# A macaron encoder block on one core: norms after the sub-layers computed in place by VectorE, four tiles at a time, and small constants loaded later

## The chip, the cores and the metric

The kernel runs on one core of one Trainium2 chip. The metric is the device time of one execution in microseconds; the median of three runs is compared, and one execution is also profiled. All data are float32 in HBM. The engines are named as in the profile: PE (TensorE), DVE (VectorE), ACT (ScalarE), POOL (GpSimd) and SP (SyncE, which here only issues DMAs).

## The reference, cut to what matters

```python
def rms_norm(x, g):
    y = x * lax.rsqrt(jnp.mean(x * x, axis=-1, keepdims=True) + EPS)
    return y * g
def swiglu(x, w_gate, w_up, w_down):
    return (jax.nn.silu(x @ w_gate) * (x @ w_up)) @ w_down
# 1024 tokens, 1024 channels, 2816 hidden
f1 = swiglu(rms_norm(h, ffn1_pre_g), ffn1_w_gate, ffn1_w_up, ffn1_w_down)
h = h + 0.5 * rms_norm(f1, ffn1_post_g)
mix = hybrid_mixer(rms_norm(h, mix_pre_g), ...)   # latent attention + dilated attention, gated, w_out
h = h + rms_norm(mix, mix_post_g)
f2 = swiglu(rms_norm(h, ffn2_pre_g), ffn2_w_gate, ffn2_w_up, ffn2_w_down)
h = h + 0.5 * rms_norm(f2, ffn2_post_g)
```

## The kernel before, in words

The 1024 tokens are eight tiles of 128 rows, t0 to t7. Every float32 product is made of three fp32r products (high by high, high by low, low by high), so each operand exists as a rounded "high" part and a "low" rest. Both FFNs use a seven-product Strassen scheme, so the input to gate and up is seven blocks of 512 tokens by 512 channels: four quarters and sums of them.

**The norms.** `prenorm` squares a tile on ACT with a running sum, makes 1/sqrt of the mean on POOL in two tiny instructions (`rstd_steps`: `var` L309, `rstd` L311), and scales the tile by that and by the gain (L453). How many of the 1024 columns DVE scales is the constant PRE1, PREM or PRE2 (768, 768 or all); the others are scaled by ACT (L459) and multiplied by the gain on POOL (L460). `postnorm` loads the residual, squares y on ACT (L501), multiplies y by the gain into a new tile `xn` (L490; the first columns on POOL, by the tables POOL1, POOLM and POOL2, the others on DVE), and then adds `xn` times rstd to the residual on DVE (L514). At two of the three places `prenorm` of the next sub-layer follows at once on the same tile; `norm_tok` lets two tiles through this pair at a time.

**Transposes.** A normed tile is transposed by PE in groups of four 128x128 pieces into one PSUM bank (L428), then ACT rounds it to `xh` (L432) and DVE makes the rest `xl` (L433), which frees the bank. There are four such banks; products use them too. For the FFNs, `XS.put` makes the sums of token halves on DVE (L416) when a tile of the second half arrives, into two `xt` tiles, and these are transposed as well. A second-half tile thus costs four L416 and five groups of transposes, a first-half tile two groups.

**What sets the order.** The program is written by generators that ask a planner (`Plan`) for an engine with an estimated duration and a rank; the planner runs its own clock and calls the code that emits each instruction. The tile framework then lists the instructions by engine, each engine runs its list in order, and every load is on SP's one queue. Loads that depend on nothing late come far ahead of where the text has them.

**Places that the change touches.** `begin` loads x and spawns the norms of the first FFN: tile 0, then 1 to 3, then 4 to 7 after a wait of 12 units of the planner's clock. `last_evac` (L1171) adds the last two products of an FFN's down projection to the accumulator `acc`; `post1` then runs the two norms into the mixer's input. `merge` makes the output projection (evacuated at L2560 into `y`) and `tail` runs the norms into the second FFN. `post2` is the last norm, whose result goes to the output. `tables`, `latent`, `dilated` and `merge` load small constants: 16 KB of masks and frequencies (`cst`), 4 KB of positions (`posi`, 4-byte pieces), the gains of the latent norms (`gq_home`), selection matrices (`sels`) and the gate bias (`bg`).

```python
        m = split_at
        spawn(on_dve(0, 512, scaled[0]), rank)
        if m > 512:
            spawn(on_dve(512, m, scaled[1]), rank)
        if m < D:
            spawn(on_pool(m, D, scaled[1]), rank)
```

Of the kernel before, what the change touches and what calls it, by code (L numbers as in the profile page):

```python
# [107 lines left out]
PRE1, PREM, PRE2 = 768, 768, D  # L108
POOL1, POOLM, POOL2 = [512] * 8, [384] * 8, [512] * 4 + [1024, 768, 512, 512]
# [4 lines left out]
EARLY = 4  # L114
W0 = 4
# [106 lines left out]
def _build(tc, es, a, consts, out, dbg):  # L222
# [44 lines left out]
    def act(n, fn):  # L267
        return ("act", 0.04 + n * 0.00088, fn)
# [87 lines left out]
    class XS:  # L356
# [25 lines left out]
        def put(self, t, xn, scaled, rank):  # L382
# [15 lines left out]
            else:  # L398
# [14 lines left out]
                tt = [slot([P, 2, 512], name="xt") for _ in range(2)]  # L413
                t1, t2, t3, t4 = tt[0][:, 0, :], tt[0][:, 1, :], tt[1][:, 0, :], tt[1][:, 1, :]
# [21 lines left out]
    def prenorm(src, g, X, t, rank, split_at, xn=None):  # L436

        bx, rs = [], []

        def sq():  # L440
            sq_ = slot([P, D], name="xn") if xn is None else xn
            ssq = small([P, 1], name="ssq")
            A.activation(sq_, src, AF.Square, accum_out=ssq)
            bx.extend((sq_, ssq))

        yield act(D + 100, sq)
        yield from rstd_steps(bx[1], D, rs)
        xn = bx[0]
        m = split_at
        scaled = [Event(), Event((m > 512) + (m < D))]  # L450

        def on_dve(c0, c1, ev):
            yield dve(c1 - c0, lambda: V.scalar_tensor_tensor(  # L453
                xn[:, c0:c1], src[:, c0:c1], rs[0], g()[:, c0:c1], op0=ALU.mult, op1=ALU.mult,
            ))
            plan.set(ev)

        def on_pool(c0, c1, ev):
            yield act(c1 - c0, lambda: A.mul(xn[:, c0:c1], src[:, c0:c1], rs[0]))  # L459
            yield pool(c1 - c0, lambda: G.tensor_mul(xn[:, c0:c1], xn[:, c0:c1], g()[:, c0:c1]))  # L460
            plan.set(ev)

        spawn(on_dve(0, 512, scaled[0]), rank)
        if m > 512:
            spawn(on_dve(512, m, scaled[1]), rank)
        if m < D:
            spawn(on_pool(m, D, scaled[1]), rank)
        yield from X.put(t, xn, scaled, rank)
# [4 lines left out]
    def postnorm(y, g, res_src, dst, t, box, junk, pool_cols, parts=1):  # L473
# [10 lines left out]

        m = pool_cols(t)
        gained = Event((m > 0) + (m < D))

        def gain_of(cols, eng):
            def write():
                eng.tensor_mul(xn[:, cols], y[:, cols], g()[:, cols])  # L490

            n = cols.stop - cols.start
            yield (pool if eng is G else dve)(n, write)
            plan.set(gained)

        xn = slot([P, D], name="xn")
        box.append(xn)
# [6 lines left out]
        if m:  # L504
            spawn(gain_of(slice(0, m), G), 0)
        if m < D:
            spawn(gain_of(slice(m, D), V), 8)
        yield act(D + 100, sq)
        yield from rstd_steps(bx[0], D, rs)
        yield gained  # L510
        n = D // parts
        for q in range(parts):
            cs = slice(n * q, n * q + n)
            yield dve(n, lambda: V.scalar_tensor_tensor(res[:, cs], xn[:, cs], rs[0], res[:, cs], op0=ALU.mult, op1=ALU.add))  # L514
            spawn(store(dst[t * P : (t + 1) * P, cs], res[:, cs], 512 // parts), 6)
# [708 lines left out]
    def begin():  # L1224
        def one(t):
            bx = []

            def ld():
                xt = slot([P, D], name="x")
                load(xt, a["x"][t * P : (t + 1) * P, :])  # L1230
                bx.append(xt)

            yield dma(512, ld)
            yield gains0
            yield from prenorm(bx[0], lambda: gb["g1"], X1, t, 3, PRE1)
# [6 lines left out]
        yield 12.0  # L1242
# [5 lines left out]
    norm_tok = Tokens(2)  # L1248

    def post1(y, t):  # L1250
# [8 lines left out]
        yield from postnorm(y, lambda: gb["p1"], a["x"], h1, t, bx, lambda: gb["j1"], POOL1.__getitem__)  # L1259
        yield from prenorm(bx[0], lambda: gb["gm"], Xm, t, 3, PREM, bx[1])  # L1260
# [8 lines left out]
    def tables():  # L1269
# [3 lines left out]
        def fetch():  # L1273
            load(cst[:, P:], consts[:, C_MJ:C_END])
            posi = keep([P, NT], I32, "posi")
            load(posi, a["positions"][0:1, :].rearrange("o (t p) -> p (o t)", p=P))
            bx.posi = posi
# [319 lines left out]
    def latent():  # L1597
# [3 lines left out]
        def lg():  # L1601
            load(gq[:, 0:384], a["q_norm_g"][0:1, :].broadcast_to([P, 384]))
# [723 lines left out]
    def dilated():  # L2326
# [3 lines left out]
        def ld():  # L2330
            dc.sel = keep([P, 2, P], F32, "sels")
            load(dc.sel, consts[:, C_SEL:C_MJ].rearrange("p (c n) -> p c n", c=2))
            dc.b1 = slot([P, 3, 256], name="b1")
            load(dc.b1, consts[:, C_B1:C_B23].rearrange("p (n c) -> p n c", c=256))
            dc.b23 = gq_home[:, 0:512].rearrange("p (n c) -> p n c", c=256)
# [118 lines left out]
    def merge():  # L2454
        yield ob_done
        bg = keep([P, 16], F32, "bg")
        yield dma(10, lambda: load(bg, a["b_gate"][0:1, :].rearrange("o (c p) -> p (o c)", p=P)))
# [106 lines left out]
        def tail(y, t, ev):  # L2564
# [3 lines left out]
            yield from postnorm(y, lambda: gb["pm"], h1, h2, t, bx, lambda: gb["jm"], POOLM.__getitem__)  # L2568
            yield from prenorm(bx[0], lambda: gb["g2"], X2, t, 3, PRE2, bx[1])
# [50 lines left out]
    def post2(y, t):  # L2620
# [5 lines left out]
        yield from postnorm(y, lambda: gb["p2"], h2, out, t, [], lambda: gb["j2"], POOL2.__getitem__, 2 if t == NT - 1 else 1)  # L2626
# [40 lines left out]
```

## Time and profile before

| what | value |
|---|---|
| time, median of 3 runs | 2434.36 us (2431.82 to 2435.98) |
| time of the profiled execution | 2432.88 us |
| its span, first to last instruction | 2430.7 us |
| PE, DVE, ACT, POOL busy | 94%, 66%, 43%, 32% of the span |
| mean granted TensorE clock | 0.974 |
| instructions | 30689 |
| moved by DMA | 350.17 MB, mean 144 GB/s |

The profile is of one execution. Engines are busy when an instruction runs on them; the granted clock is a share of full speed, 1.0 being the higher of the two levels. A bracket at the end of a line of the timeline is the idle time of the engine before that instruction and who ended it. The profiled execution took 2432.88 us, of which 2430.7 us are the span.

### The profile page before, as it was taken

How to read it: one execution, taken by the hardware profiler on the slowest of the kernel's cores; microseconds unless marked ns; L12 is line 12 of the kernel's file. 1: busy time of each engine (PE TensorE's matmuls, PEld its weight loads, DVE VectorE, ACT ScalarE, POOL GpSimd, SP SyncE). 2: the span in 40 equal slices, each digit the busy share in tenths (PEclk: the TensorE clock that was granted, in tenths of full speed). 3: DMA queues.
4: the chain of work that ended last, by engine and by line, in shares of the span. 5: the costliest groups of instructions: out<-in, count | busy, mean ns of one | idle time of the engine just before them, and what ended most of it. 6: DMA issues, size and time to landing. Idle time of an engine off the chain costs nothing. (4 is left out here: it accounts for less than half of the span.)

```text
span 2430.7 us, 30689 instructions
## 1 busy us (share of the span) xinstructions
PE 2294.6 (94%) x11096; PEld 1920.7 (79%) x11096; DVE 1609.8 (66%) x2669; ACT 1044.0 (43%) x1952; POOL 784.1 (32%) x592
## 2 busy tenths in 40 slices
PE   6999999999979999999998898988979999999997
PEld 4788888788869987888886777776868888887885
DVE  7877878875672105666666766347787778778658
ACT  6233434431153336666655545454433334344111
POOL 2000000354274555756532322575300000006443
PEclk9999999999989999999999999999979999999998
DMA  6234434587352133122223222675533444357762
GB/s 186 83 130 139 173 127 163 195 321 254 134 173 70 62 98 100 38 72 65 61 82 90 79 73 85 194 258 180 182 108 113 163 140 173 116 197 280 259 238 104
DMA packets 197145, 350.17 MB, mean 144 GB/s; under 512 B 32577, under 2 KB 112961, under 8 KB 196481
## 3 DMA queue, kind: packets, MB, share of 16 engines
q1 hardware_dynamic: 196992, 348.21, 42.6%
q8 instruction: 87, 1.43, 0.2%
q14 instruction: 66, 0.53, 0.1%
HBM read 234.78 MB, written 113.38 MB: 143 GB/s over the span
## 5 line engine op out<-in xcount | busy, mean ns | idle before, releaser
L706 PE MATMUL s<-xh,wt 128*128 128x512 f32 x1408 | 453.8, 393 | 10.2 <-DVE uu L807 9.0
L524 POOL TENSOR_TENSOR wdb<-rawd,wdb 128x1024 fp32r<-128x1024 f32 x34 | 87.3, 2567 | 892.4 <-ACT wdb L523 889.3
L706 PE MATMUL b<-xh,wt 128*128 128x512 f32 x1056 | 345.7, 394 | 0.7 <-ACT xh L432 0.6
L706 PEld LDWEIGHTS s<-xh,wt 128*128 128x128 f32 x1408 | 266.2, 189 | 69.8 <-DVE uu L807 10.7
L706 PE MATMUL s<-xl,wt 128*128 128x512 f32 x704 | 275.7, 392 | 0.0
L706 PEld LDWEIGHTS b<-xh,wt 128*128 128x128 f32 x1056 | 200.9, 190 | 44.0 <-ACT xh L432 1.0
L706 PE MATMUL b<-xl,wt 128*128 128x512 f32 x528 | 207.7, 393 | 0.9 <-DVE xl L433 0.9
L1134 PE MATMUL b<-wdb,ha 128*128 128x512 f32 x864 | 202.5, 389 | 0.0
L1134 PE MATMUL s<-wdb,ha 128*128 128x512 f32 x816 | 190.5, 389 | 0.0
L1134 PEld LDWEIGHTS b<-wdb,ha 128*128 128x128 f32 x864 | 162.4, 188 | 33.8
L1134 PEld LDWEIGHTS s<-wdb,ha 128*128 128x128 f32 x816 | 153.1, 188 | 31.8
L1495 PE MATMUL b<-xh,wh 128*128 128x512 f32 x384 | 162.7, 424 | 1.4 <-DVE o L2016 0.8
L1966 POOL TENSOR_TENSOR p<-p,rd 128x1024 f32<-128x1024 f32 x64 | 122.5, 1923 | 117.7 <-DVE rd L1963 112.5
L706 PEld LDWEIGHTS s<-xl,wt 128*128 128x128 f32 x704 | 133.3, 189 | 27.4
L1495 PE MATMUL b<-xl,wh 128*128 128x512 f32 x384 | 153.2, 399 | 0.0
L675 ACT CAST wt<-s 128x512 fp32r<-128x512 f32 x176 | 104.2, 617 | 113.9 <-DVE s L635 59.0
L1495 PE MATMUL b<-xh,wl 128*128 128x512 f32 x384 | 152.9, 398 | 0.0
L524 POOL TENSOR_TENSOR wdb<-td,wdb 128x1024 fp32r<-128x1024 f32 x40 | 108.1, 2706 | 109.7 <-ACT wdb L523 98.6
L428 PE MATMUL b<-cst,p 128*128 128x128 f32 x768 | 107.2, 280 | 22.2 <-DVE ptd L433 14.9
L524 POOL TENSOR_TENSOR wl<-raw,wh 128x512 fp32r<-128x512 f32 (+3 forms) x88 | 110.0, 1267 | 53.5 <-ACT wh L523 46.5
L428 PEld LDWEIGHTS b<-cst,p 128*128 128x128 f32 x768 | 90.1, 143 | 40.0 <-DVE ptd L433 17.5
L676 DVE TENSOR_TENSOR wt<-s,wt 128x512 fp32r<-128x512 f32 x176 | 117.9, 684 | 5.4 <-ACT wt L675 5.1
(298 smaller groups left out, 4989.8 us busy)
## 6 DMA issues: line engine op xcount, KB each, us to landing
hs_d<-hl SPq DMA_DIRECT2D x112, 512.0 KB
ha<-hs_d SPq DMA_DIRECT2D x56, 1024.0 KB
raw<-in_ffn_w_gate_dram SPq DMA_DIRECT2D x48, 512.0 KB
raw<-in_ffn_w_up_dram SPq DMA_DIRECT2D x48, 512.0 KB
rawd<-in_ffn_w_down_dram SPq DMA_DIRECT2D x44, 512.0 KB
raw<-in_w_in_dram SPq DMA_DIRECT2D x28, 512.0 KB
h<-res SPq DMA_DIRECT2D x16, 512.0 KB
lg_d<-lg SPq DMA_DIRECT2D x32, 256.0 KB
```

Source lines behind the costliest of these rows:

```text
L428: T.transpose(b[:rows, i * P : (i + 1) * P], src(i), ident)
L524: yield pool(n, lambda: G.tensor_sub(lo, src, hi))
L675: yield act(512, lambda: A.copy(w[:, 0], src))
L676: yield dve(512, lambda: V.tensor_sub(w[:, 1], src, w[:, 0]))
L706: T.matmul(out(), l, r, start=(first and k == 0 and n == 0), stop=(k == 3 and n == 2), skip_group_check=True,)
L1134: T.matmul(ps, l, r, start=(fresh and n == 0), stop=(n == 5), skip_group_check=True)
L1495: T.matmul(bs.ps, l, r, start=(part == 0 and n == 0), stop=(part == 7 and n == 2))
L1966: yield pool(S, lambda: G.tensor_tensor(bx.p, bx.p, bx.rd.broadcast_to([P, S]), op=ALU.mult))
```

## The change

The norms lose their shares for POOL and ACT. `postnorm` multiplies y by the gain in place, all 1024 columns on DVE, after the square on ACT has read y; the tile that was y then takes the next `prenorm`'s result, so no `xn` tile is taken. `prenorm` scales two halves of 512 columns on DVE. `norm_tok` goes from 2 to 4. `XS.put` writes the first and last of its four sums over the old tile and takes one `xt` tile where it took two. Five loads of small constants get a one- or two-column copy ahead of them, from data that come late, into their own destination, so that they cannot be listed early. `begin` spawns tiles 4 to 7 after 7 units in place of 12.

```diff
-PRE1, PREM, PRE2 = 768, 768, D
-POOL1, POOLM, POOL2 = [512] * 8, [384] * 8, [512] * 4 + [1024, 768, 512, 512]
+NORM = 4
...
-                tt = [slot([P, 2, 512], name="xt") for _ in range(2)]
-                t1, t2, t3, t4 = tt[0][:, 0, :], tt[0][:, 1, :], tt[1][:, 0, :], tt[1][:, 1, :]
+                tt = slot([P, 2, 512], name="xt")
+                t1, t2, t3, t4 = old[0], tt[:, 0, :], tt[:, 1, :], old[1]
...
-        def on_pool(c0, c1, ev):
-            yield act(c1 - c0, lambda: A.mul(xn[:, c0:c1], src[:, c0:c1], rs[0]))
-            yield pool(c1 - c0, lambda: G.tensor_mul(xn[:, c0:c1], xn[:, c0:c1], g()[:, c0:c1]))
-            plan.set(ev)
...
+        for n in range(2):
+            spawn(scale(512 * n, 512 * n + 512, scaled[n]), rank)
...
-        if m:
-            spawn(gain_of(slice(0, m), G), 0)
-        if m < D:
-            spawn(gain_of(slice(m, D), V), 8)
+        def gain_of():
+            yield dve(D, lambda: V.tensor_mul(y, y, g()))
+            plan.set(gained)
+
         yield act(D + 100, sq)
+        spawn(gain_of(), 2)
...
-            yield dve(n, lambda: V.scalar_tensor_tensor(res[:, cs], xn[:, cs], rs[0], res[:, cs], op0=ALU.mult, op1=ALU.add))
+            yield dve(n, lambda: V.scalar_tensor_tensor(res[:, cs], y[:, cs], rs[0], res[:, cs], op0=ALU.mult, op1=ALU.add))
...
-        yield 12.0
+        yield 7.0
...
-    norm_tok = Tokens(2)
+    norm_tok = Tokens(NORM)
...
+            seen = X1.blk[6][0].bitcast(F32)[:, 0, 0:1]
+            V.tensor_copy(cst[:, P : P + 1], seen)
             load(cst[:, P:], consts[:, C_MJ:C_END])
             posi = keep([P, NT], I32, "posi")
+            V.tensor_copy(posi[:, 0:1], seen)
...
+            V.tensor_copy(gq[:, 383:385], gb["gm"][:, 0:2])
...
-            load(dc.sel, consts[:, C_SEL:C_MJ].rearrange("p (c n) -> p c n", c=2))
             dc.b1 = slot([P, 3, 256], name="b1")
             load(dc.b1, consts[:, C_B1:C_B23].rearrange("p (n c) -> p n c", c=256))
+            V.tensor_copy(dc.sel[:, 0, 0:1], dc.b1[:, 0, 0:1])
+            load(dc.sel, consts[:, C_SEL:C_MJ].rearrange("p (c n) -> p c n", c=2))
...
+            V.tensor_copy(bg[:, 0:1], dc.sel[:, 0, 0:1])
```

SP at the start of the program, before. The first `x` row is t3, the others are t4 to t7; `raw` are weights of the first FFN.

```order
L1230 DMA x_108<-in_x_dram 128x1024
L519 DMA raw_117<-in_ffn_w_gate_dram 128x8x128
L1274 DMA cst<-in_consts_dram 128x32
L1276 DMA posi<-in_positions_dram 128x8x1
L1602 DMA gq_home<-in_q_norm_g_dram 128x384
L519 DMA raw_163<-in_ffn_w_up_dram 128x8x128
L1230 DMA x_183<-in_x_dram 128x1024
L1230 DMA x_197<-in_x_dram 128x1024
L1603 DMA gq_home<-in_kv_norm_g_dram 128x256
L1230 DMA x_211<-in_x_dram 128x1024
L1230 DMA x_230<-in_x_dram 128x1024
```

The same place in the changed program, from the fourth tile of x on:

```order
L1209 DMA x_108<-in_x_dram 128x1024
L1209 DMA x_117<-in_x_dram 128x1024
L1209 DMA x_135<-in_x_dram 128x1024
L1209 DMA x_159<-in_x_dram 128x1024
L1209 DMA x_178<-in_x_dram 128x1024
L498 DMA raw_190<-in_ffn_w_gate_dram 128x8x128
L498 DMA raw_228<-in_ffn_w_up_dram 128x8x128
L498 DMA raw_259<-in_ffn_w_gate_dram 128x8x128
```

The eight tiles of x stand together, ahead of all weights, and none of the small loads stands near them: `cst` and `posi` come after three and six larger weight loads, `gq_home` some 165 rows later, `sels` and `bg` some 350.

DVE at the end of the first FFN, before. `acc` are the accumulators of two halves (each tile needs two L1171), L490 the gain, L514 the residual, L453 the next norm.

```order
L1171 TENSOR_TENSOR acc_3857<-acc_3857,b_5068 128x512
L490 TENSOR_TENSOR xn_5168<-acc_3847,p_738_5058 128x512
L1171 TENSOR_TENSOR acc_3857<-acc_3857,b_5076 128x512
L514 SCALAR_TENSOR_TENSOR res_5132<-xn_5168,rstd_5187,res_5132 128x1024
L1171 TENSOR_TENSOR acc_3870<-acc_3870,b_5085 128x512
L453 SCALAR_TENSOR_TENSOR xn_5144<-res_5122,rstd_5210,gm_5093 128x512
L1171 TENSOR_TENSOR acc_3870<-acc_3870,b_5095 128x512
L453 SCALAR_TENSOR_TENSOR xn_5144<-res_5122,rstd_5210,gm_5093 128x256
L1171 TENSOR_TENSOR acc_3881<-acc_3881,b_5103 128x512
```

The changed program there (L1150 is the old L1171, L483 the gain, L493 the residual, L451 the next norm, L432 the old L433):

```order
L493 SCALAR_TENSOR_TENSOR res_5124<-acc_3839,rstd_5179,res_5124 128x1024
L1150 TENSOR_TENSOR acc_3882<-acc_3882,b_5126 128x512
L1150 TENSOR_TENSOR acc_3882<-acc_3882,b_5138 128x512
L493 SCALAR_TENSOR_TENSOR res_5136<-acc_3852,rstd_5192,res_5136 128x1024
L1150 TENSOR_TENSOR acc_3891<-acc_3891,b_5154 128x512
L1150 TENSOR_TENSOR acc_3891<-acc_3891,b_5169 128x512
L451 SCALAR_TENSOR_TENSOR acc_3820<-res_5104,rstd_5201,gm_5075 128x512 x2
L451 SCALAR_TENSOR_TENSOR acc_3829<-res_5114,rstd_5225,gm_5075 128x512 x2
L451 SCALAR_TENSOR_TENSOR acc_3839<-res_5124,rstd_5232,gm_5075 128x512 x2
L432 TENSOR_TENSOR xl_5238<-b_5240,xh_5236 128x4x128
L451 SCALAR_TENSOR_TENSOR acc_3852<-res_5136,rstd_5248,gm_5075 128x512 x2
```

All sixteen additions to the accumulators now stand ahead of the first L451, with the gains and residuals of t0 to t3 between them; then come four L451 pairs together, then eight `xl`. Before, the L453 of t0 and t1 stood between the additions, and tiles went on in pairs. PE's list follows: 32 transposes, 96 products, 32 transposes where there were 16, 48, 16, 48, 16, 48.

PE where the second FFN's products meet the first transposes of t4 to t7, before. `wo` by `mt` is the output projection, L706 the second FFN's products.

```order
L285 MATMUL b_15267<-wo_15106,mt_15065 128x512 x3
L706 MATMUL b_15284<-xh_14662,wt_14972 128x512
L706 MATMUL b_15284<-xl_14663,wt_14972 128x512
L706 MATMUL b_15284<-xh_14662,wt_14972 128x512 x2
L706 MATMUL b_15284<-xl_14663,wt_14972 128x512
```

The changed program from the end of its twelfth such product to the transposes (L685 is the old L706, L427 the old L428):

```order
L685 MATMUL b_15137<-xh_14606,wt_15099 128x512 x2
L685 MATMUL b_15137<-xl_14607,wt_15099 128x512
L685 MATMUL b_15137<-xh_14606,wt_15099 128x512
L427 MATMUL b_15342<-cst,y_14591 128x128 x4
L427 MATMUL b_15351<-cst,y_14656 128x128 x4
```

Behind the last output projection stood 36 L706, four transposes and twelve more L706; now twelve stand there, and 36 have gone ahead of the last 48 products of the output projection. Outside these stages and the last norm the lists of PE are the same, instruction for instruction, but for buffer numbers.

## Rows read from the trace of the kernel before

**Rows 1.** Parts 1 and 2 of the page: busy time by engine; clock in 40 slices.

```profile
PE 2294.6 (94%) x11096; PEld 1920.7 (79%) x11096; DVE 1609.8 (66%) x2669; ACT 1044.0 (43%) x1952; POOL 784.1 (32%) x592
...
PEclk9999999999989999999999999999979999999998
```

**Rows 2.** Stretches: length, busy PE, PEld, DVE, ACT, POOL; clock, DMA share, GB/s.

```profile
0.00:58.00 58.00, 36.40 (x162) 26.79 (x162) 45.56 (x76) 36.47 (x68) 14.63 (x28) 0.91 0.62 185
58.00:450.00 392.00, 391.05 (x1723) 322.71 (x1722) 303.15 (x517) 146.99 (x263) 0.00 (x0) 1.00 0.40 139
...
664.00:750.00 86.00, 68.97 (x393) 61.87 (x392) 63.68 (x73) 40.34 (x77) 60.73 (x63) 0.92 0.43 143
...
1660.00:1705.00 45.00, 36.03 (x160) 29.04 (x159) 37.88 (x37) 26.73 (x47) 33.77 (x29) 0.92 0.61 207
...
1763.00:1798.00 35.00, 21.35 (x93) 16.14 (x92) 31.45 (x48) 13.71 (x25) 5.13 (x6) 0.61 0.45 157
...
2391.50:2430.70 39.20, 22.82 (x97) 17.60 (x95) 32.48 (x36) 9.21 (x16) 24.01 (x24) 0.84 0.43 161
```

**Rows 3.** Timeline of SP's queue at the start: start us, us, instruction.

```profile
7.49 3.68 SPq L1602 DMA_DIRECT2D gq_home<-in_q_norm_g_dram  x1
...
11.69 1.18 SPq L1230 DMA_DIRECT2D x<-in_x_dram  x2
```

**Rows 4.** DVE and PE at the start: timeline, and one group of DVE's.

```profile
10.50 1.60 DVE L453 SCALAR_TENSOR_TENSOR xn<-x,rstd,g 128x512 f32<-128x512 f32 x2 [1.99 <-POOL rstd L311]
...
57.62 0.60 PE L428 MATMUL b<-cst,xt 128*128 128x128 f32 x4
...
61.28 0.17 DVE L1286 CAST posf<-posi 128x8 f32<-128x8 int32 x1
...
L453 DVE SCALAR_TENSOR_TENSOR xn<-x,rstd,g 128x512 f32<-128x512 f32 x8 | 8.2, 1025 | 8.9 <-POOL rstd L311 8.9
```

**Rows 5.** Timeline of POOL, DVE and PE at the end of the first FFN.

```profile
666.60 0.69 DVE L1171 TENSOR_TENSOR acc<-acc,b 128x512 f32<-128x512 f32 x1
...
675.88 1.28 DVE L514 SCALAR_TENSOR_TENSOR res<-xn,rstd,res 128x1024 f32<-128x1024 f32 x1 [0.40 <-POOL rstd L311]
...
675.94 3.48 POOL L524 TENSOR_TENSOR wl<-raw,wh 128x1024 fp32r<-128x1024 f32 x1
...
680.37 2.82 DVE L453 SCALAR_TENSOR_TENSOR xn<-res,rstd,gm 128x512 f32<-128x512 f32 x1 [2.61 <-POOL rstd L311]
...
683.85 8.73 PE L285 MATMUL b<-wdb,hp 128*128 128x512 f32 x30 [3.69 <-DVE acc L1171]
...
747.35 2.48 DVE L433 TENSOR_TENSOR xl<-b,xh 128x512 fp32r<-128x512 f32 x4
```

**Rows 6.** A group by shape, 664 to 752 us: count, busy us, mean ns.

```profile
L524 POOL TENSOR_TENSOR wc<-raw,wc 128x768 fp32r<-128x768 f32 x4 | 7.9, 1998 | 0.0
```

**Rows 7.** The mixer's end: a group (1660 to 1705 us), then the timeline.

```profile
L453 DVE SCALAR_TENSOR_TENSOR xn<-res,rstd,g 128x512 f32<-128x512 f32 x8 | 13.0, 1660 | 2.4 <-POOL rstd L311 2.3
...
1752.99 0.39 PE L706 MATMUL b<-xh,wt 128*128 128x512 f32 x1
...
1757.48 3.95 POOL L311 TENSOR_TENSOR rstd<-var,neg_half 128x1 f32<-128x1 f32 x1
...
1782.44 1.09 PE L428 MATMUL b<-cst,xn 128*128 128x128 f32 x4 [8.12 <-DVE xn L453]
...
1793.45 0.78 PE L706 MATMUL b<-xh,wt 128*128 128x512 f32 x1
```

**Rows 8.** Timeline of DVE in the last norm: first addition, last residual.

```profile
2393.07 0.69 DVE L1171 TENSOR_TENSOR acc<-acc,b 128x512 f32<-128x512 f32 x1
...
2425.86 1.42 DVE L514 SCALAR_TENSOR_TENSOR res<-xn,rstd,res 128x512 f32<-128x512 f32 x2 [0.72 <-POOL rstd L311]
```

**Rows 9.** By line and by tile: b1's load; the first use of sels.

```profile
L2334 SPq DMA_DIRECT2D b<-in_consts_dram x1: 385/385/385, 1181.7 to 1181.7; - x1
...
L2169 PE MATMUL b<-z,sels x16: 218/275/323, 1238.1 to 1513.4; 128*128 128x64 f32 x16
```

More of the change, by code (lines that the diff above doesn't have):

```diff
@@ L434, in transpose_split, with prenorm @@
         plan.release(B1)
-    def prenorm(src, g, X, t, rank, split_at, xn=None):
+    def prenorm(src, g, X, t, rank, xn=None):
         bx, rs = [], []
@@ L448, in prenorm, with scale @@
         xn = bx[0]
-        m = split_at
-        scaled = [Event(), Event((m > 512) + (m < D))]
-        def on_dve(c0, c1, ev):
+        scaled = [Event(), Event()]
+        def scale(c0, c1, ev):
             yield dve(c1 - c0, lambda: V.scalar_tensor_tensor(
@@ L456, in on_dve @@
             plan.set(ev)
-        def on_pool(c0, c1, ev):
-            yield act(c1 - c0, lambda: A.mul(xn[:, c0:c1], src[:, c0:c1], rs[0]))
-            yield pool(c1 - c0, lambda: G.tensor_mul(xn[:, c0:c1], xn[:, c0:c1], g()[:, c0:c1]))
-            plan.set(ev)
-        spawn(on_dve(0, 512, scaled[0]), rank)
-        if m > 512:
-            spawn(on_dve(512, m, scaled[1]), rank)
-        if m < D:
-            spawn(on_pool(m, D, scaled[1]), rank)
+        for n in range(2):
+            spawn(scale(512 * n, 512 * n + 512, scaled[n]), rank)
         yield from X.put(t, xn, scaled, rank)
@@ L471, in store, with postnorm @@
         yield dma(kb, lambda: load(dst, src))
-    def postnorm(y, g, res_src, dst, t, box, junk, pool_cols, parts=1):
+    def postnorm(y, g, res_src, dst, t, box, junk, parts=1):
         bx, rs = [], []
@@ L483, in postnorm @@
         res = box[0]
[L485 to L497, printed above, removed]
+        box.append(y)
+        gained = Event()
         def sq():
@@ L502, in sq @@
             bx.append(ssq)
-        if m:
-            spawn(gain_of(slice(0, m), G), 0)
-        if m < D:
-            spawn(gain_of(slice(m, D), V), 8)
+        def gain_of():
+            yield dve(D, lambda: V.tensor_mul(y, y, g()))
+            plan.set(gained)
         yield act(D + 100, sq)
+        spawn(gain_of(), 2)
         yield from rstd_steps(bx[0], D, rs)
@@ L1234, in one @@
             yield gains0
-            yield from prenorm(bx[0], lambda: gb["g1"], X1, t, 3, PRE1)
+            yield from prenorm(bx[0], lambda: gb["g1"], X1, t, 3)
         spawn(one(0), 0)
@@ L1258, in post1 @@
         bx = []
-        yield from postnorm(y, lambda: gb["p1"], a["x"], h1, t, bx, lambda: gb["j1"], POOL1.__getitem__)
-        yield from prenorm(bx[0], lambda: gb["gm"], Xm, t, 3, PREM, bx[1])
+        yield from postnorm(y, lambda: gb["p1"], a["x"], h1, t, bx, lambda: gb["j1"])
+        yield from prenorm(bx[0], lambda: gb["gm"], Xm, t, 3, bx[1])
         plan.release(norm_tok)
@@ L2456, in merge, with ld @@
         bg = keep([P, 16], F32, "bg")
-        yield dma(10, lambda: load(bg, a["b_gate"][0:1, :].rearrange("o (c p) -> p (o c)", p=P)))
+        def ld():
+            V.tensor_copy(bg[:, 0:1], dc.sel[:, 0, 0:1])
+            load(bg, a["b_gate"][0:1, :].rearrange("o (c p) -> p (o c)", p=P))
+        yield dma(10, ld)
         m_tok, w_tok, wd_tok = Tokens(4), Tokens(1), Tokens(4)
@@ L2567, in tail @@
             bx = []
-            yield from postnorm(y, lambda: gb["pm"], h1, h2, t, bx, lambda: gb["jm"], POOLM.__getitem__)
-            yield from prenorm(bx[0], lambda: gb["g2"], X2, t, 3, PRE2, bx[1])
+            yield from postnorm(y, lambda: gb["pm"], h1, h2, t, bx, lambda: gb["jm"])
+            yield from prenorm(bx[0], lambda: gb["g2"], X2, t, 3, bx[1])
             plan.release(norm_tok)
@@ L2625, in post2 @@
         yield gains2
-        yield from postnorm(y, lambda: gb["p2"], h2, out, t, [], lambda: gb["j2"], POOL2.__getitem__, 2 if t == NT - 1 else 1)
+        yield from postnorm(y, lambda: gb["p2"], h2, out, t, [], lambda: gb["j2"], 2 if t == NT - 1 else 1)
     def second():
```

## The prediction, made before the changed kernel was run

> **What bounds the kernel now.** I read the page first. PE is busy for 2294.6 of 2430.7 us, and the clock falls only in a few slices [rows 1]: time can come only from stretches where PE waits or runs at the lower level of its clock. The busy time by stretches shows them [rows 2]. From 58 to 450 us PE is busy for 391.05 of 392 us, 1723 matmuls, 0.227 us each; nothing done there by other engines can show. At the start 21.6 of 58 us are idle, at the end of the first FFN 17.0 of 86, in the output projection 9.0 of 45, at the entry to the second FFN 13.7 of 35 at a clock of 0.61, and in the last norm PE is done before DVE. In all five DVE is the busiest or near it: 45.56 of 58, 63.68 of 86, 37.88 of 45, 31.45 of 35, 32.48 of 39.2 us. These are the five stages where norms stand between two pieces of PE's work. Everything else keeps its order, so the sum is made over these stages.
>
> **Prices.** On DVE, 512 columns cost 0.60 us in a row of such instructions (four in 2.48 us) and 1024 columns 1.28 us alone [rows 5]; I take 1.2 in a row, and 0.64 for half of a scaled tile. The new gain of 1024 columns does not exist in the trace; between twice the 0.60 and the 1.28 there is little to choose. These are times without POOL beside them. With it, the same 512 columns take 1.025 us in the mean at the start [rows 4], 1.66 us at the end of the mixer [rows 7], and once 2.82 us [rows 5]. So the shares that POOL loses shorten what stays on DVE, but POOL's weight splits (3.48 us [rows 5], 2.00 us [rows 6]) and its tiny rstd instructions stay.
>
> **The start: 0.** Eight tiles of x come together. Before, t4 and t5 were issued at 11.69 us, behind small loads, one of which held the queue for 3.68 us [rows 3]. But the data are not the limit: DVE is. The second tile's scaling starts at 10.50 us [rows 4]; from there to the last `xl` of the first FFN's input the changed list of DVE has 64 instructions, at 0.62 us 39.7 us, so the input is complete at 50.2. PE pays for this: its list now puts 88 transposes ahead of the first product, which starts when DVE is 48 instructions on, at 40.3. Then come 20 products and 24 transposes, 4.5 and 3.6 us at full clock (transposes at the 0.15 of four in 0.60 [rows 4]) and twice that at the lower level: PE is through between 48.4 and 56.5 us, but not before the input is. I take 51. At 57.6 us, where PE had become continuous with 49 products done (counted in its old list) [rows 4], it would have 20 + 6.6/0.227 = 49. That is 0; the ends are -2.1 and +5.7 us.
>
> **End of the first FFN: -4.** The first L1171 starts at 666.60 [rows 5]. DVE's list then has 16 L1171 and 2 more additions (10.8 us), four gains and four residuals (9.6), eight L453 (5.1) and eight `xl` (4.8): 30.3 us, with 2 us of waits for squares and rstd the first half of the mixer's input is ready at 699. The second half is 9.6 + 5.1 + 4.8 = 19.5 us: 718.5 if POOL is silent, or 726 if two `wc` splits and one `wl` (2.0 + 2.0 + 3.48) hold DVE up in full, as they are listed just there. PE runs through from about 2 us before that. What PE then lacks to where it stood when the old `xl` ended (747.35 + 2.48 = 749.8 [rows 5]) are 72 products of 256 columns, 96 of 384 and 12 transposes: 8.2 + 16.3 + 1.3 = 25.8 us by 0.227 per 512. So 742.3 or 749.8, against 749.8: -7.5 or 0. I take -4, since the splits overlap only partly with the gains. What goes: the stall of 3.69 us that came when DVE waited 2.61 us for an rstd behind a 3.48 us split [rows 5], because no L453 now stands ahead of an addition. What is late next: the first half, as four tiles must be through before PE's first transposes. Ends: -10.5, if half of the 6.9 us that the clock of 0.92 costs over 86 us [rows 2] goes too, and +4.6, if each of the eight L453 pairs waits another 0.6 us for its rstd, as DVE does at L514 for 0.40.
>
> **Output projection and entry to the second FFN: -2.5.** In the first half DVE's eight L453 took 13.0 us where 5.1 would do [rows 7], partly for POOL's gain shares, which go, partly for its splits, which stay; I give PE back half of its 9.0 idle us [rows 2], -4.5. At the entry, PE ended the output projection at 1752.99 and stood 8.12 us for a tile whose norm had no token [rows 7]; with four tokens that wait goes. But 36 products of the second FFN are now listed ahead of the last 48 of the output projection, 36 x 0.227 = 8.2 us, so y is complete that much later. From there DVE has two residuals, a gain, eight L453, sixteen L416, twenty `xl` and two more: with waits for squares some 34 us, where it took 40.5 from 1752.99 to the first product after the transposes at 1793.45 [rows 7]. 8.2 later and 6.5 shorter is +1.7; another 0.3 for rstds gives +2. Together -2.5, ends -9 (all of the projection's idle time) and +5.
>
> **The last norm: -0.5.** From 2393.07 [rows 8] DVE has 18 additions (10.8 us), eight gains and eight residuals (19.2): 30.0 us, so 2423.1, plus 0.6 for the first square and three waits of 0.72 for rstds, as the last one had: 2425.9. Before, it ended at 2425.86 + 1.42 = 2427.3. That is -1.4; as the last stores now come closer together, I take -0.5, with ends -4 and +2.
>
> **The copies: 0.** Five copies of one or two columns, at most the 0.17 us of a small cast [rows 4], and each makes SP wait for DVE. The loads behind `cst` and `posi` are third and later units' weights, hidden under the continuous stretch; `sels` follows `b1`, issued at 1181.7, and is first used at 1238.1 [rows 9]. If that cover were gone, a load and a copy would show, some 3 us.
>
> **Sum.** 0 - 4 - 2.5 - 0.5 = -7 us. The sum is against the profiled execution, 2432.88 us (span 2430.7), which lies 1.5 us under the median of 2434.36. So 2426 us. About 0.2%, 4.9 us, is what a measurement of this kernel can tell: faster is below 2429.5, slower above 2439.2.
>
> **Rivals.** *Nothing gained.* DVE carries what POOL and ACT carried and the groups of four only move the waits: PE stands longer before the first transposes of each group and shorter later. For it: DVE was the busiest engine in each stage already [rows 2]. Against: it was busy partly because POOL held it. With the weak ends (0 at the first FFN, 0 at the output projection, +2 at the second FFN, 0 at the end): 2435.
>
> *The rstds starve: slower.* One `rstd` took 3.95 us [rows 7] where I take 0.6 for one with DVE idle: it stood through a row of DVE instructions that read two SBUF tiles. Now DVE runs more such rows: gains, residuals and scalings back to back. POOL's rstd then comes late, and DVE itself waits for it at the next residual. There are five groups of tiles (two after each of two sub-layers, and the end) in each of which two rstds can be on the path; if half of the ten lose 3.4 us, that is 17 us, less the gain of 7: 2443. It decides from a mean loss of 0.7 us for each of the ten. Against it: once DVE waits, POOL is free to go on, and additions and `xl`, which read PSUM, stand between in the first halves. The Trainium skill, SBUF — State Buffer, section "Who interferes with whom", says that a VectorE instruction with two SBUF inputs and a GpSimd instruction that reads SBUF exclude each other, and that the one that comes second waits for the whole of the first. The 3.95 us show a wait through more than one instruction; by the rule's single wait, at 1.28 us, the ten would lose 12.8 us at most, and this rival would end at 2438.7.
>
> *All of the freed time arrives.* Without POOL's shares the scalings fall back to 0.64 us, chains end early and the clock stays up. Half of the 17.0 and all of the 9.0 idle us, and 3.5 of the clock's: 2432.88 - 8.5 - 9 - 3.5 = 2412. For it: 1.66 against 0.64 us [rows 7]. Against: the splits stay.
>
> **How the numbers follow.** The forecast, 2419 to 2431, has 0.39; nothing gained 0.27; starving 0.16; all arrives 0.18. Faster by over 0.2% is 0.18, most of the forecast (0.33) and a little of the second case: 0.53. Within 0.2%: 0.06 + 0.23 = 0.29. Slower: 0.16 and 0.02 of the second: 0.18. The range is 2410 to 2441 us: it reaches to the cases on both sides and leaves out the sums of all ends, 2407 and 2450.
>
> **What would show it.** Right: the scalings of 512 columns at 0.6 to 0.75 us in all stages; the input of the first FFN complete near 50 us and PE's first product near 40; no stall for an addition between 664 and 690 us; POOL free of `xn`. Wrong: `rstd` at over 1.4 us in the mean, DVE idle before residuals for more than 2 us a group, PE waiting over 8 us ahead of the first transposes at the end of the first FFN, or a time above 2431 with stages at or above their old length. A time under 2419 would mean that the splits on POOL cost DVE less than I let them.

## The result, and the profile after

The changed kernel takes 2418.99 us (median of four runs, 2418.78 to 2423.56) against 2435.17 of before in the same comparison: a ratio of 0.9941, interval 0.9923 to 0.9958, faster by 0.6%. The forecast was 2426 (2410 to 2441), faster. The profiled execution took 2419.11 us with a span of 2417.3: 13.4 us less span than before, where the sum said 7.

Part 1 of the page after, and the clock:

```profile
PE 2293.5 (95%) x11096; PEld 1920.7 (79%) x11096; DVE 1605.0 (66%) x2675; ACT 1038.5 (43%) x1936; POOL 736.5 (30%) x552
...
PEclk9999999999989999999999999999989999999999
```

DVE is no busier than before, though it has taken over columns from POOL and ACT [rows 1]: POOL lost 48 us, and DVE got back in shorter instructions what it took on: its busy time is 1605.0 us, 1609.8 before. Busy time by stretches of the kernel after, with the columns of [rows 2], each stretch set to hold about the same work:

```profile
0.00:58.00 58.00, 39.87 (x167) 29.93 (x168) 45.70 (x80) 34.11 (x61) 8.53 (x20) 1.00 0.49 167
58.00:450.00 392.00, 391.10 (x1723) 322.81 (x1722) 302.22 (x515) 147.70 (x264) 1.30 (x1) 1.00 0.41 142
...
662.00:745.00 83.00, 69.05 (x421) 62.23 (x421) 58.87 (x70) 39.29 (x76) 47.34 (x51) 0.90 0.43 149
1648.00:1692.00 44.00, 39.04 (x174) 31.28 (x173) 37.44 (x44) 27.90 (x50) 18.96 (x21) 0.92 0.66 229
1750.00:1785.00 35.00, 21.72 (x99) 16.85 (x98) 33.74 (x49) 17.54 (x31) 7.45 (x15) 0.76 0.39 144
2378.00:2417.30 39.30, 24.40 (x108) 19.88 (x106) 33.46 (x41) 9.21 (x16) 11.22 (x16) 0.86 0.27 107
```

The end of the first FFN still holds 14 us in which PE stands, at a clock of 0.90. To see what each stage gained, one needs points that both programs pass. By-line views give the first and last start of such instructions; here of before:

```profile
L706 PE MATMUL s<-xl,wt x704: 387/389/628, 71.7 to 2202.9; 128*128 128x512 f32 x176
...
L1171 DVE TENSOR_TENSOR acc<-acc,b x32: 673/675/689, 666.6 to 2422.5; 128x512 f32<-128x512 f32 x32
...
L428 PE MATMUL b<-cst,p x768: 270/272/477, 927.9 to 1541.0; 128*128 128x128 f32 x192
...
L285 PE MATMUL b<-wo,mt x384: 387/389/776, 1594.1 to 1752.8; 128*128 128x512 f32 x192
...
L706 PE MATMUL b<-xh,wt x1056: 387/389/795, 20.0 to 2182.5; 128*128 128x512 f32 x176
...
L1134 PE MATMUL b<-wdb,ha x864: 387/389/508, 462.3 to 2391.3; 128*128 128x512 f32 x173
```

and the same of after:

```profile
L685 PE MATMUL s<-xl,wt x704: 387/389/628, 70.3 to 2191.9; 128*128 128x512 f32 x176
...
L1150 DVE TENSOR_TENSOR acc<-acc,b x32: 672/682/689, 664.1 to 2402.4; 128x512 f32<-128x512 f32 x32
...
L427 PE MATMUL b<-cst,p x768: 270/273/474, 922.3 to 1538.1; 128*128 128x128 f32 x192
...
L284 PE MATMUL b<-wo,mt x384: 387/389/792, 1589.7 to 1754.0; 128*128 128x512 f32 x192
...
L685 PE MATMUL b<-xh,wt x1056: 387/389/776, 41.5 to 2173.5; 128*128 128x512 f32 x176
...
L1113 PE MATMUL b<-wdb,ha x864: 387/389/628, 460.9 to 2380.2; 128*128 128x512 f32 x173
```

They cut the span into four stages that the change touches, used in the table of experiments too. **A**, the start: to the first `s<-xl,wt`. **B**, the end of the first FFN: from the first of the last additions (L1171) to the first transposition of `p` in the attention. **C**, output projection and entry to the second FFN: from the first `b<-wo,mt` to the last `b<-xh,wt`. **D**, the last norm: from the last `b<-wdb,ha` to the end. The rest is the same instructions in the same order, but for the copies and the loads behind them.

| stage | forecast | measured |
|---|---|---|
| A, start | 0 | 70.3 - 71.7 = -1.4 |
| B, end of the first FFN | -4 | 258.2 - 261.3 = -3.1 |
| C, output projection, second FFN's entry | -2.5 | 583.8 - 588.4 = -4.6 |
| D, last norm | -0.5 | 37.1 - 39.4 = -2.3 |
| rest | 0 | -2.0 |
| span | -7 | -13.4 |

B looks as forecast. The experiments show that this is luck: it is the sum of a gain of 13.5 us and a loss of 10.4, each some three times the forecast.

### The profile page after: what moved, and what is told of

Same layout as the page of the kernel before. It is cut to its first block, busy times and chain, and to the rows that moved or that the text cites. A ratio compares the mean times of both kernels' runs of the same rounds, so it can differ in the third digit from the quotient of the medians.

```text
span 2417.3 us, 30606 instructions
## 1 busy us (share of the span) xinstructions
PE 2293.5 (95%) x11096; PEld 1920.7 (79%) x11096; DVE 1605.0 (66%) x2675; ACT 1038.5 (43%) x1936; POOL 736.5 (30%) x552
## 5 line engine op out<-in xcount | busy, mean ns | idle before, releaser
L685 PE MATMUL s<-xh,wt 128*128 128x512 f32 x1408 | 451.3, 391 | 9.7 <-DVE uu L786 4.6
L685 PE MATMUL b<-xh,wt 128*128 128x512 f32 x1056 | 342.7, 392 | 2.6 <-DVE y L2549 2.6
L685 PEld LDWEIGHTS s<-xh,wt 128*128 128x128 f32 x1408 | 264.8, 188 | 68.8 <-DVE uu L786 6.0
L685 PE MATMUL s<-xl,wt 128*128 128x512 f32 x704 | 274.6, 390 | 0.1
L685 PEld LDWEIGHTS b<-xh,wt 128*128 128x128 f32 x1056 | 199.6, 189 | 44.7 <-ACT wt L638 3.1
L685 PE MATMUL b<-xl,wt 128*128 128x512 f32 x528 | 206.7, 391 | 0.0
L685 PEld LDWEIGHTS s<-xl,wt 128*128 128x128 f32 x704 | 132.5, 188 | 27.6 <-DVE xl L432 0.4
L427 PE MATMUL b<-cst,p 128*128 128x128 f32 x768 | 107.5, 280 | 21.8 <-DVE ptd L432 14.5
L427 PEld LDWEIGHTS b<-cst,p 128*128 128x128 f32 x768 | 90.0, 143 | 40.0 <-DVE ptd L432 17.1
```

Source lines behind the costliest of these rows:

```text
L427: T.transpose(b[:rows, i * P : (i + 1) * P], src(i), ident)
L685: T.matmul(out(), l, r, start=(first and k == 0 and n == 0), stop=(k == 3 and n == 2), skip_group_check=True,)
```

## The experiments

Twelve kernels ran, in groups that each shared runs of the kernel before on the same chip. Times are medians, ratios are to those runs, with 95% intervals; A to D are the change of a stage against the profile of before, in us, each from one profiled execution.

| run | what it is | us | ratio | A | B | C | D |
|---|---|---|---|---|---|---|---|
| after | the change | 2418.99 | 0.9941 [0.9923, 0.9958] | -1.4 | -3.1 | -4.6 | -2.3 |
| e1 | before + new start and copies | 2434.81 | 1.0003 [0.9992, 1.0014] | +1.8 | -0.2 | +0.2 | -0.3 |
| e2 | before + all shares to DVE | 2413.67 | 0.9921 [0.9905, 0.9937] | +0.9 | -8.9 | -2.1 | -3.7 |
| e3 | e2 + four tokens | 2428.40 | 0.9978 [0.9967, 0.9989] | 0.0 | -3.4 | +6.1 | -4.1 |
| e4 | after, two tokens | 2410.98 | 0.9905 [0.9888, 0.9922] | -2.4 | -13.5 | -3.6 | -2.5 |
| e5 | e4 with the old start | 2407.44 | 0.9889 [0.9872, 0.9907] | -1.5 | -13.6 | -6.6 | -2.5 |
| e6 | before + gain to DVE | 2419.28 | 0.9939 [0.9924, 0.9954] | +0.9 | -5.3 | -5.6 | -3.8 |
| e7 | before + scaling to DVE | 2430.35 | 0.9984 [0.9974, 0.9995] | -0.8 | -3.4 | +1.7 | +0.1 |
| e8 | after, one token | 2435.98 | 1.0003 [0.9993, 1.0013] | -2.1 | +4.1 | +2.4 | -3.3 |
| e9 | e5, mixer splits on DVE | 2402.90 | 0.9870 [0.9850, 0.9889] | -1.9 | -18.9 | -7.1 | -2.6 |
| e10 | e5 with three tokens | 2414.59 | 0.9917 [0.9902, 0.9932] | -0.6 | -9.0 | -0.1 | -2.5 |
| e11 | e5, last gain in a tile of its own | 2412.23 | 0.9898 [0.9879, 0.9917] | -1.6 | -11.8 | -3.5 | -3.4 |
| e12 | e9, four tokens from the output projection on | 2401.19 | 0.9872 [0.9854, 0.9890] | -2.3 | -19.8 | -6.2 | -2.6 |

How far a single stage can be trusted is seen in stages that a run does not touch: e7 has +1.7 in C without an edit there, and the dilated stage from 1234 to 1544 us, in which the only edit of any run is one copy ahead of a load, differs by -0.9 to +5.4 us between these profiles (-0.9 to +3.5 in runs without the copy). B itself is -13.5, -13.6 and -11.8 in e4, e5 and e11, whose norms are alike there. A difference of 2 us in one stage says little, one of 8 says much.

### e1: the start and the copies alone

The kernel before with the diff's `yield 7.0` and its five copies, nothing else.

> The kernel before with the start of the change alone: the copies ahead of the five small loads, and tiles 4 to 7 of x spawned after 7 units. My theory: the start and the copies give about what the profile of after shows there, 1.4 us sooner at PE's first s<-xh,wt product on xl, so 2433 to 2434, the same within 0.2%. Rival, the start is the main part: below 2427, with the later stages as long as before. Rival, the copies cost: above 2440.

2434.81 us, 1.0003: no change, and the copies cost nothing that shows. The earlier loads of x are worth nothing that shows, alone or with two tokens: e5, which has the old start, is not slower than e4.

### e2: all shares to DVE, two tokens

```diff
-PRE1, PREM, PRE2 = 768, 768, D
-POOL1, POOLM, POOL2 = [512] * 8, [384] * 8, [512] * 4 + [1024, 768, 512, 512]
+PRE1, PREM, PRE2 = D, D, D
+POOL1, POOLM, POOL2 = [0] * 8, [0] * 8, [0] * 8
```

> The kernel before with all shares of the norms on DVE (768, 768, D become D; POOL's columns all 0), still two tokens, xn tiles, old start. My theory: shares alone give about half of the gain, since POOL no longer holds DVE: 2426 to 2430. Rival, order: without four tokens the shares only load DVE more, and the time is 2433 or more. Rival, shares are everything: 2420 to 2422.

2413.67 us: 20 us faster than before. Two lines of constants bring at least what the change does; the 5 us by which e2 is ahead of it are at the edge of the noise (the intervals overlap). My 2426 to 2430 allowed for a third of it; even the rival that gave everything to the shares, 2420 to 2422, was too careful.

### e3: four tokens on top of e2

```diff
-    norm_tok = Tokens(2)
+    norm_tok = Tokens(4)
```

> As e2, with four tokens in place of two; xn tiles and the old start kept. My theory: 2420 to 2424, that is the whole change but for the start. Rival, the place of y and xt (fewer tiles taken from the pool) matters: as e2 or slower, since the third and fourth tile would wait for a free tile.

2428.40 us, 15 us slower than e2. My theory fell. The rival said this for want of tiles; that isn't shown, since the order of PE changes with the tokens too. That the loss is in B (5.5 us) and in C (8.2) is. The changed kernel has four tokens as well, with y and the sums in place, and is 9.4 us faster than e3; its C is 10.7 us shorter. So at the output projection four tokens are bearable only with the results in place.

### e4: the change with two tokens

```diff
-NORM = 4
+NORM = 2
```

> The changed kernel with two tokens in place of four. My theory: tokens are worth about half of the later gain, so 2424 to 2428, and PE waits again at the entry to the second FFN for a tile that has no token (8 us before). Rival, tokens are worth nothing: 2419. Rival, tokens are everything: 2432.

2410.98 us: the four tokens cost the change 8 us. It is the opposite of what I expected, and none of the three cases. The loss is at the end of the first FFN: B is -13.5 in e4 and -3.1 in the change. PE's timeline there, first of after (start us, length us, instruction; in brackets the idle time ahead of it):

```profile
662.50 21.92 PE L284 MATMUL b<-wdb,hp 128*128 128x512 f32 x96
685.86 2.64 PE L427 MATMUL b<-cst,acc 128*128 128x128 f32 x16 [1.45 <-DVE acc L451]
689.78 0.66 PE L427 MATMUL b<-cst,acc 128*128 128x128 f32 x4 [1.27 <-DVE xl L432]
691.70 2.38 PE L427 MATMUL b<-cst,acc 128*128 128x128 f32 x12 [1.26 <-DVE xl L432]
693.72 0.56 PE L284 MATMUL b<-wh,xh 128*128 128x256 f32 x1
...
707.49 0.63 PE L427 MATMUL b<-cst,acc 128*128 128x128 f32 x4 [1.03 <-DVE acc L451]
710.16 1.09 PE L427 MATMUL b<-cst,acc 128*128 128x128 f32 x4 [2.04 <-DVE acc L451]
713.09 1.94 PE L427 MATMUL b<-cst,acc 128*128 128x128 f32 x8 [1.84 <-DVE acc L451]
720.06 3.50 PE L427 MATMUL b<-cst,acc 128*128 128x128 f32 x16 [5.03 <-DVE xl L432]
```

Then of e4:

```profile
681.67 1.53 PE L284 MATMUL b<-wdb,hp 128*128 128x512 f32 x6
683.04 1.03 PE L427 MATMUL b<-cst,acc 128*128 128x128 f32 x8
684.31 0.38 PE L284 MATMUL b<-wh,xh 128*128 128x256 f32 x1 [0.24 <-ACT xh L431]
684.53 0.28 PE L284 MATMUL b<-wl,xh 128*128 128x256 f32 x1
684.65 0.60 PE L427 MATMUL b<-cst,acc 128*128 128x128 f32 x4
```

With four tokens PE works off all 32 transposes of the first half before its first product of the mixer, and stands three times ahead of them and among them, 4.0 us in all; then its products are done before the next four tiles are, and it stands 9.9 us more. With two it goes from the last product of the FFN into the transposes without a gap, needs eight of them for its first product of the mixer, and has that at 684.3 instead of 693.7 us (1.2 of these 9.4 us come from ahead of the stage). Over the stretch from 662 to 745 us, in the columns of [rows 2], e4 is:

```profile
662.00:745.00 83.00, 75.33 (x475) 69.56 (x474) 61.56 (x74) 41.35 (x82) 41.66 (x52) 0.98 0.44 140
```

PE stands 7.7 us there, where it stands 14.0 in the changed kernel, and its clock is 0.98 in place of 0.90. So 6.3 us of the loss are standing; the lower clock that came with it can account for the other 4.

### e5: and with the old start

e4 without the five copies and with `yield 12.0`: norms on DVE, norms and sums in place, two tokens, and nothing else.

> The changed kernel with two tokens and the old start (no copies, 12 units): shares on DVE and in place, nothing else. e1 says that the start is worth 0, e2 that shares alone are worth 20 us. My theory now: 2411 to 2414, as e2 and e4, the start and the place of y each being worth 3 us at most. Rival, the start is worth something only together with the other parts: above 2415.

2407.44 us (0.9889 against e4's 0.9905, intervals that overlap): below the range that I gave, the rival fell, and it is faster than the change by half a per cent. B is -13.6 again, where e2 with tiles of their own had -8.9. Two things differ there: in e2 sixteen transposes stand ahead of the first product of the mixer, in e4 eight; and in e2 POOL makes two splits (3.48 and 3.10 us) among the first tiles, where e4 has none. What of the in-place form brings these 5 us was not separated.

### e6 and e7: which share held DVE

Each is one of e2's two lines: e6 sets POOL's columns of the gain to 0, e7 the scaling to D.

> The kernel before with POOL's columns of the gain all 0 and the shares of the scaling kept (768, 768, D). POOL's gain runs while DVE scales and adds. My theory: most of e2's 20 us are here, since POOL's gain lies in all four places: 2416 to 2422. Rival, the scaling's way over ACT and POOL was the slow part: 2428 or more.

> The kernel before with the scaling all on DVE (768, 768 become D) and POOL's columns of the gain kept. It touches the start and the end of the first FFN only. My theory: 2428 to 2434, a gain of 0 to 5 us at the end of the first FFN. Rival, the scaling's way over ACT and POOL was the slow part: 2420 or less.

2419.28 and 2430.35 us, -15.5 and -4.5 against their shared 2434.83. The two add up to e2's -20, and the gain is three quarters of it, as expected. It is the part that lies in B, C and D alike. They also settle which share made PE's stall of 3.69 us at the end of the first FFN [rows 5]; the same products in e7 (POOL's gain kept), then in e6 (POOL's gain gone):

```profile
681.26 9.79 PE L285 MATMUL b<-wdb,hp 128*128 128x512 f32 x30 [3.68 <-DVE acc L1171]
```

```profile
686.02 1.69 PE L285 MATMUL b<-wdb,hp 128*128 128x512 f32 x6 [0.75 <-DVE acc L1171]
```

In both POOL makes two `wl` splits there; in e6 the first starts at 670.46 us and in e7 at 673.37, behind two gains, and only in e7 does DVE wait (2.61 us) for the rstd that stands behind it.

### e8 and e10: one and three tokens

> The changed kernel with one token. Theory, the fewer tiles are in flight, the sooner PE gets its first transposes and products at the end of the first FFN, but one tile at a time leaves DVE waiting for squares and rstds: 2412 to 2422, between two and four tokens. Rival, the order by lumps of tiles is all that counts, so one is better than two: 2408 or less. Rival, one chain at a time bounds the entry to the second FFN: above 2425, most of it there.

> e5 with three tokens. Theory, PE's list at the end of the first FFN is what the number of tokens decides: with three, 24 transposes stand ahead of the first products of the mixer, so the stage lies between that with two (13.6 us shorter than before) and that with four (3.1 shorter): 2411 to 2416. Rival, two and three are alike and only four is bad, since four tiles take all four PSUM banks of the transposes: 2406 to 2409. Rival, an odd number breaks the halves of 256 tokens, which PE takes two tiles at a time: 2417 or more.

One token: 2435.98 us, the whole gain lost, B at +4.1. PE starts on the mixer as early as in e4, but the tiles come too slowly; at 747.8 and 761.1 us it still waits 3.5 and 3.3 us for one. My range for it was too low, and the rival that had the time looked for the loss at the second FFN: against e4, B is 17.6 us longer and C 6.0. Three: 2414.59 us, B at -9.0, between -13.6 and -3.1 as the theory had it; PE's timeline shows 24 transposes there before the first product. That it gains nothing in C is not explained. So at this place the best number is two.

### e9: the mixer's splits on DVE

```diff
+    def split_v(src, hi, lo, n):
+        yield act(n, lambda: A.copy(hi, src))
+        yield dve(n, lambda: V.tensor_sub(lo, src, hi))
...
-                yield from split(rs[c], wh, wl, 1024)
+                yield from split_v(rs[c], wh, wl, 1024)
...
-                yield from split(bx[0], *hl, m * wide)
+                yield from split_v(bx[0], *hl, m * wide)
```

> e5 with the low parts of the latent weights (wc, wcl) and of the first two groups of filler weights (wl) made by DVE in place of POOL. In e4 three residuals beside such splits took 2.82, 3.23 and 3.24 us where one alone takes 1.28, 5.4 us in all. Theory, the splits on POOL are what is left of the cost at the end of the first FFN: the stage 2 to 5 us shorter, 2402 to 2406. Rival, DVE is full there and the splits cost it what they save: 2406 to 2409, the stage as long as in e5 within 2 us. Rival, the splits delay the norms: above 2411.

2402.90 us, as the theory had it (its interval and e5's overlap, the times of the runs do not), B at -18.9, 5.3 shorter than e5. DVE's residuals from 664 to 740 us (count, busy us, mean ns), first of e4, then of e9:

```profile
L493 DVE SCALAR_TENSOR_TENSOR res<-acc,rstd,res 128x1024 f32<-128x1024 f32 x8 | 15.7, 1966 | 0.8 <-POOL rstd L310 0.4
```

```profile
L493 DVE SCALAR_TENSOR_TENSOR res<-acc,rstd,res 128x1024 f32<-128x1024 f32 x8 | 10.1, 1278 | 0.1
```

and busy time by engine in the same stretch of e9:

```profile
664.00:740.00 76.00, 73.29 (x460) 67.77 (x459) 60.93 (x79) 38.53 (x75) 22.74 (x40) 0.98 0.47 154
```

DVE runs 79 instructions there where e4 runs 70 in the same stretch. Its splits cost it 7.3 us; its eight residuals alone give back 5.6, and its scalings give back 0.6 and wait 3.5 us less for rstds. So here what POOL did beside DVE cost DVE about as much as doing it itself. PE is busy for 73.3 of 76 us, where it was for 68.3 in e4.

### e11: the last gain in a tile of its own

```diff
-            yield dve(D, lambda: V.tensor_mul(y, y, g()))
+            yield dve(D, lambda: V.tensor_mul(xn, y, g()))
...
+        xn = slot([P, D], name="xn") if own else y
+        if own:
+            spawn(gain_of(), 8)
         yield act(D + 100, sq)
-        spawn(gain_of(), 2)
+        if not own:
+            spawn(gain_of(), 2)
...
```

> e5 with the gain of the last norm written to a tile of its own, listed before the square is done, as before; all on DVE. In e2 and e6, which have that, the last stage is 3.7 and 3.8 us shorter than before, in e4 and e5 2.5. Theory, in place the gain has to wait for the square: 1 us, 2406.5, hardly to be told from e5. Rival, DVE has other work in that wait: 2407.4, and the stage as in e5 within 0.3 us.

D is -3.4 against -2.5, which looks like the 1 us of the theory; but e8, which has the gain in place, has -3.3, and the time is 2412.23 (2402.29 to 2413.92), slower than e5 in the median. The runs scatter more than the effect, and it stays open.

### e12: four tokens for the output projection alone

```diff
     def merge():
         yield ob_done
+        plan.release(norm_tok, 2)
```

> e9 with two tokens at the end of the first FFN and four from the output projection on, as in the change. From PE's first output projection product to the last gate or up product b<-xh,wt of the second FFN, after is 4.6 us shorter than before, e4 3.6, e5 6.6 and e9 7.1. Theory, at the second FFN's entry the wait for a token that four take away (7.5 us in e5) is paid back by the products that go ahead, so four tokens are worth 0 there and the whole loss of four was at the end of the first FFN: 2401 to 2405. Rival, the wait was worth its 7.5 us: 2395 to 2398. Rival, four tokens are bad in both places: 2408 or more.

2401.19 us, C at -6.2 against -7.1: with results in place, four tokens are worth nothing here. PE's timeline of e9 (two tokens), then of e12 (four), where it waits for tiles of the second half:

```profile
1755.18 1.09 PE L427 MATMUL b<-cst,y 128*128 128x128 f32 x4 [7.47 <-DVE y L451]
1757.63 1.09 PE L427 MATMUL b<-cst,y 128*128 128x128 f32 x4 [1.37 <-DVE y L451]
```

```profile
1741.81 0.63 PE L427 MATMUL b<-cst,y 128*128 128x128 f32 x4 [3.41 <-DVE y L451]
...
1749.04 1.08 PE L427 MATMUL b<-cst,y 128*128 128x128 f32 x4 [4.82 <-DVE y L451]
```

The wait of 7.47 us goes, and two of 8.23 together are there in its place. This version and e9 are the fastest of the study, 1.3% ahead of before.

## Why the prediction was right, and where not

The direction and the range held, and the time came 7 us below the forecast (2419 for 2426). Not all of the reasons held, and that stage B came out near its forecast is luck. The ends of some stages do not follow from their own terms (at the start, 48.4 to 56.5 us against the 51 taken, with the input at 50.2, give -0.8 and +5.5, not -2.1 and +5.7); the range does not rest on them.

**Prices.** Scalings of 512 columns without POOL: 744 ns at the start after, beside 0.64 assumed and 1.025 us before [rows 4]. At the second FFN's entry they have 744 ns too. At the end of the first FFN they take 0.99 us in the mean, and at the mixer's end 1.00, where they took 1.66 [rows 7]: POOL's splits stayed, as the prediction let them. So the 0.6 to 0.75 us that it asked for is there in two of four stages. Gains and residuals of 1024 columns have 1.22 and 1.28 us alone, as taken.

**The start: 0.** PE's first product was forecast at 40.3 us and came at 41.5; the input complete at 50.2 and it was at 51.5 (last `xl`). -1.4 us in this profile, -1.5 with the old start (e5), and no change in time by e1. Right, and for the reason given: DVE sets it, not the loads; from 10.62 us, where it starts on the second tile, it runs without a pause to 45.8.

**End of the first FFN: -4.** Measured -3.1, and the steps came as worked out: the first half ready 31.7 us after the first addition (32.4 forecast), the second half at 724.9, where 718.5 to 726 less the 2.5 us of earlier start would be 716 to 723.5. DVE needs 29.1 us for the second half, where 19.5 were counted without POOL: three pairs of its gains and scalings that run beside splits are some 6 us longer than alone, and it waits 2.5 us for rstds, which the sum had left to its upper end. But the step that names what goes is wrong. "Because no L453 now stands ahead of an addition" credits the four tokens with the end of the 3.69 us stall. In e4 the scalings stand among the additions again, and the stall is not there; e6 and e7 show that it goes with POOL's gain. Shares and in-place form are worth 13.5 us here (8.9 with the shares alone, e2); the four tokens take 10.4 of these away. "What is late next: the first half, as four tiles must be through before PE's first transposes" named the very mechanism, but it got no price of its own: that was to be had by asking what the same list would take with two tiles at a time.

**Output projection and second FFN's entry: -2.5.** The last addition to y starts at 1755.5 in the kernel after, 1755.3 before: over stage C up to there +4.6, where -4.5 + 8.2 = +3.7 was forecast. The rest was mis-sized: 34 us from the output projection's end (1754.4) to the first product after the transposes, and it took 29.1. Of the sixteen L416 and twenty `xl` that I counted, only eleven and fourteen stand ahead of that product in DVE's list; the other eleven, 6.6 us, come behind it. The four tokens do take the wait of 8.12 us [rows 7] away, and two others take its place: 3.41 and 4.82 us ahead of transposes of `y`, in this kernel as in e12. This credit to the tokens was empty.

**The last norm: -0.5.** -2.3. The forecast was -1.4 for DVE and 0.9 back for the stores. DVE took 30.7 us from the first addition at 2382.0 to the end of the last residual at 2412.7, of which it waited 1.0 us for PE (30.0 of work were counted); before it took 34.2 [rows 8]. What I added for rstds was not there:

```profile
2405.37 2.48 DVE L493 SCALAR_TENSOR_TENSOR res<-acc,rstd,res 128x1024 f32<-128x1024 f32 x2
2407.76 1.22 DVE L483 TENSOR_TENSOR acc<-acc,p 128x1024 f32<-128x1024 f32 x1
2408.90 3.80 DVE L493 SCALAR_TENSOR_TENSOR res<-acc,rstd,res 128x1024 f32<-128x1024 f32 x4
```

No residual waits for an rstd: the three waits of 0.72 us, 2.2 in all, are the term that failed, as DVE always has another tile's gain to do meanwhile. Of its 3.5 us the stores give back 1.2: from the last residual to the end of the span are 4.6 us where there were 3.4.

**The copies: 0.** Held, by e1: 1.0003.

**The rivals.** *Nothing gained* fell. *The rstds starve* did not come: an rstd takes 0.74 us in the mean where it took 0.67, and one took 2.61 (below), but DVE's scalings waited only 5.6 us for rstds in the whole program, and its residuals 0.7. *All of the freed time arrives*, 2412 us, is what the change does without the four tokens: e4 has 2411. The time lies between this rival and the forecast because the four tokens give 8 us back. The sign "a time under 2419 would mean that the splits on POOL cost DVE less than I let them" misleads: at 2418.99 the splits cost DVE all that was allowed, as B's second half and e9 show.

**Not forecast.** -2.0 us in the rest. It has no edit in it but the copies, and over all runs it differs from before by -5.2 to +3.6 us; what part of this is the clock (last section) was not separated.

## What to carry to other kernels

Where two engines read the same memory, count a share given to the slower one as time on the faster one too: taking POOL's gain away gave DVE more columns, left its busy time as it was (1607 us in e6, 1610 before) and made the kernel 15 us faster, and moving splits to DVE brought another 4 to 5. More tiles in flight are not better by themselves: where one engine's list is written in groups, the group's size decides when the next stage gets its first operand, and it has a best value (here two of one, two, three and four). A term that comes out near its forecast can be two wrong ones of opposite sign; undoing one part at a time shows it.

## What the runs showed of the hardware that was not expected

An rstd of one column stood through more than one DVE instruction. POOL, then DVE, after:

```profile
703.96 2.61 POOL L310 TENSOR_TENSOR rstd<-var,neg_half 128x1 f32<-128x1 f32 x1
```

```profile
703.74 1.27 DVE L493 SCALAR_TENSOR_TENSOR res<-acc,rstd,res 128x1024 f32<-128x1024 f32 x1
704.94 1.21 DVE L483 TENSOR_TENSOR acc<-acc,p 128x1024 f32<-128x1024 f32 x1
706.60 0.75 DVE L451 SCALAR_TENSOR_TENSOR acc<-res,rstd,gm 128x512 f32<-128x512 f32 x1 [0.45 <-POOL rstd L310]
```

It began at 703.96 us, just after the residual had, and ended at 706.57, 0.42 us after the gain had; alone it takes 0.55. The rstd of 3.95 us before, from 1757.48 to 1761.43 [rows 7], stood through six DVE instructions:

```profile
1757.26 0.75 DVE L453 SCALAR_TENSOR_TENSOR xn<-res,rstd,g 128x512 f32<-128x512 f32 x1
1757.92 1.29 DVE L676 TENSOR_TENSOR wt<-s,wt 128x512 fp32r<-128x512 f32 x2
1759.12 0.69 DVE L642 TENSOR_TENSOR s<-raw,s 128x512 f32<-128x512 f32 x1
1759.73 0.68 DVE L638 TENSOR_TENSOR s<-raw 128x512 f32<-128x512 f32 x1
1760.33 0.69 DVE L416 TENSOR_TENSOR xt<-xn,xo 128x512 f32<-128x512 f32 x1
```

It ended 0.41 us after the last of them; DVE made a pause of 1.60 us there. The Trainium skill, SBUF — State Buffer, "Who interferes with whom", has the second instruction wait for the whole of the first; waits through two and through six instructions are more than that, and here the measurement decides.

The clock fell at different places in the same list of instructions. Ahead of 468 us PE stood once for 4.39 us in the kernel before, and the stretch from 450 to 480 us has a granted clock of 0.89; after the change it stood twice there, 2.46 and 2.74 us, and the clock stayed at 1.00. In the dilated stage it was the other way round; first before, then after, about the same part of the list:

```profile
1530.00:1550.00 20.00, 17.84 (x98) 14.86 (x97) 9.95 (x10) 8.77 (x14) 9.90 (x5) 1.00 0.19 66
```

```profile
1525.00:1545.00 20.00, 17.97 (x85) 14.80 (x86) 9.26 (x10) 7.63 (x11) 7.09 (x4) 0.83 0.16 57
```

Busy for the same share of the time, PE went through 98 matmuls in the one and 85 in the other. At 17.84 us for 98, the 13 are worth some 2.4 us (an estimate). How much of what the stages of single profiles differ by comes from such places was not separated.
